# Block-sum DMAs of a hybrid decoder layer: half-size pieces at projection slots, copies on ScalarE's queue

## The chip, the cores and the metric

The kernel runs on one core of a Trainium2 chip. The metric is the device time of one execution in microseconds. The kernel before took 2511.54 us, the median of 2 runs (2511.51 to 2511.57).

The core has five engines that work side by side, each through its own instructions in order: TensorE (PE in the profile; PEld is its weight loads), VectorE (DVE), ScalarE (ACT), GpSimd (POOL) and SyncE (SP, which only issues DMAs here). DMAs are issued from the queue of an engine; the transfers themselves run on 16 DMA engines.

## The reference

One decoder layer over 2048 tokens of width 1024, with 16 learned meta tokens in front:

```python
u = _rmsnorm(h, norm_pre[layer])
proj = u @ w_in                      # split into 12 parts
att = _swa_sink_branch(a_q, a_k, a_v, attn_sinks)      # window 128, rotary, sinks
y_a = (att * silu(a_z)) @ w_attn_out
cell = _mlstm_cell(m_q, m_k, m_v, m_i, m_f)            # chunkwise recurrence
hm = _head_layernorm(sigmoid(m_o) * cell, head_norm)
y_m = (hm * silu(m_z)) @ w_mlstm_out
merged = sigmoid(g_a) * y_a + sigmoid(g_m) * y_m
h = h + _rmsnorm(merged @ w_out, norm_post[layer])
```

The code above is shortened; the projections are float32 and are computed to that accuracy from split operands (below).

## The kernel before

The kernel has two parts. The **projection part** takes the tokens in two halves of 1024 (`for c in range(NHALF)`, line 820). For each half it goes through 14 entries of `PLAN` (line 828): "A" entries project queries, keys and values of a group of heads for 8 blocks of 128 tokens, "F" entries project features (q and k of the mLSTM, or the gate `ga`), "M" entries project values and output gates of an mLSTM head. Every float32 operand is split into a high and a low part (`whi`, `wlo` for weights, `un` for tokens), and each product is three matmuls; `load_w` (line 217) loads the weights of an entry as `wraw` from SyncE's queue and splits them on ScalarE and VectorE (lines 229 to 235). A projection of one block is 24 matmuls. After every 6 of them, and at the end, it calls `slot()` (line 318), which counts a clock and lets waiting chains (attention blocks, mLSTM blocks, gates) put their next instructions in. When the queue of attention blocks is too long, `slot()` is also called without matmuls between. TensorE's order is the order of the code; the other engines' order is set by a scheduler that takes instructions by priority when it believes that their inputs are ready.

The **product part** (from line 966) computes six products of 2048x1024 by 1024x1024 (gates `az`, `mz`, `gm`, then `att`, `hm`, `out`), each by Winograd's form of Strassen's scheme: 7 products of half-size blocks instead of 8. That needs sums of weight blocks and of token blocks, the **block sums**. They are formed in DRAM during the projection part, by DMAs alone. `weight_sums()` (line 182) makes four blocks of 1 MB for each of the six matrices (`sw_d`): a copy `cp` from the weights `wq` or from another sum, then an accumulating DMA `add` onto it. `token_sums(c)` (line 165) does five accumulating DMAs on the token blocks `uo_d[c]`. The token blocks are written by `tokens()` (line 738): for each of 8 slices of tokens the scaled slice, and for some a negated copy made on ScalarE in a staging tile `xs` of four, is stored from SyncE's queue (lines 752 and 756).

Before, copies go through SyncE's queue and additions through POOL's. A copy is preceded by a transfer of one column of the newest weight tile `wlo` into its target (line 187), so that it can't be issued before that tile exists. One step of `weight_sums` (2 or 4 transfers of 1 MB) is put in at each entry of the plan (`next(sums, None)`), one of `token_sums` at entries 4, 6 and 8. Gate maxima of a half are stored to `mr_d` (line 395), and each mLSTM block loads its row of them, broadcast to all partitions, as `mrep` (line 608) from SyncE's queue.

Of the kernel before, what the change touches and what calls it, by code (L numbers as in the profile page):

```python
# [14 lines left out]
ALU = mybir.AluOpType  # L15
# [8 lines left out]
SB = 512  # L24
# [64 lines left out]
def hybrid_layer(ctx: ExitStack, tc: tile.TileContext, x, xT, mx, mxT, gpre, w_all, wq, negs, cw, cb,  # L89
                 gbias, hnorm, gpost, rope, ident, sel, bmask, out):  # L90
    nc = tc.nc
    V, S, G, T = nc.vector, nc.scalar, nc.gpsimd, nc.tensor
# [21 lines left out]
    def f(t):  # L114
        return t.bitcast(F32)
# [27 lines left out]
    def late_consts():  # L143
        for t, src in ((sink_t, negs.partition_broadcast(128)), (bm_t, bmask), (sel_t, sel),
# [16 lines left out]
    sw_d = [[dram.tile([128, 4 * SB], F32, name=f"sw{m}{i}_d") for i in range(4)] for m in range(len(MATS))]  # L161
    op_d = {(n, c): [dram.tile([128, 4, SB], F32, name=f"op_{n}{c}{i}_d") for i in range(7)]
            for n in ("att", "hm", "mg") for c in range(SEQ // (2 * SB))}

    def token_sums(c):
        b00, b10, t2, t1, t3, b11, t4, n01 = uo_d[c]

        def add(dst, src):
            G.dma_start(out=dst, in_=src, accum_op=ALU.add, max_dma_last_dim=4096)

        add(t1, n01)
        add(t3, n01)
        add(t2, b00)
        yield
        add(t2, n01)
        yield
        add(t4, t2)
        yield

    block_w = [None]  # L180

    def weight_sums():
        for a in range(0, len(MATS), 2):
            pair = (a, a + 1)

            def cp(dst, src):
                nc.sync.dma_start(out=dst[:, 0:1], in_=f(block_w[0])[:, 0:1])
                nc.sync.dma_start(out=dst, in_=src)

            def add(dst, src):  # L190
                G.dma_start(out=dst, in_=src, accum_op=ALU.add, max_dma_last_dim=4096)

            for m in pair:
                cp(sw_d[m][2], wq[m, 0, 0])
                cp(sw_d[m][0], wq[m, 1, 1])
            yield
            for m in pair:
                add(sw_d[m][2], wq[m, 0, 1])
                add(sw_d[m][0], wq[m, 0, 1])
            yield  # L200
            for m in pair:
                cp(sw_d[m][1], sw_d[m][2])
            yield
            for m in pair:
                add(sw_d[m][1], wq[m, 1, 1])
            yield
            for m in pair:
                cp(sw_d[m][3], sw_d[m][1])
            yield
            for m in pair:  # L210
                add(sw_d[m][3], wq[m, 1, 0])
            yield

    seq = [0]
    extra = [None]
# [42 lines left out]
    with es1:  # L258
# [54 lines left out]
        clock = [0, 0]  # L313

        def spawn(gen, delay=0):
            active.append([clock[0] + delay, gen])

        def slot():
            clock[0] += 1
            if queue and clock[0] >= clock[1] and clock[0] % SLOTS == CHAIN_PHASE:  # L320
                spawn(queue.pop(0))
                clock[1] = clock[0] + gap[0]
            for ch in list(active):
                if ch[0] <= clock[0]:
                    try:
                        ch[0] = clock[0] + next(ch[1])
                    except StopIteration:
                        active.remove(ch)

        def drain(all_=False):  # L330
            while queue or (all_ and active):
                slot()
# [432 lines left out]
        def token_proj(us, o, wh, wl, w, ps=None):  # L765
            if ps is None:
                ps = ps_p.tile([128, SB], F32, name="pj")
            n = 0
            for k in range(KT):
                for a, ww in ((0, wh), (0, wl), (1, wh)):  # L770
                    T.matmul(ps[:, :w], lhsT=us[k][:, a, o:o + 128], rhs=ww[k][:, :w],  # L771
                             start=(n == 0), stop=(n == 3 * KT - 1))
                    n += 1
                    if n % SLOT == 0 and n < 3 * KT:
                        slot()
            return ps
# [25 lines left out]
        rsn = [None] * SBH  # L802
        u = [None, None]
        late = None
        sums = weight_sums()

        def first_proj(us, wh, wl, w):
            banks = [ps_p.tile([128, SB], F32, name="pj") for _ in range(2)]
# [11 lines left out]
        for c in range(NHALF):  # L820
# [7 lines left out]
            for pi, (kind, arg, cols) in enumerate(PLAN):  # L828
                w = len(cols)
                if c == 0 and pi == 0:  # L830
# [13 lines left out]
                    wh, wl = load_w(w_all, off, w, each)  # L844
                else:
                    wh, wl = load_w(w_all, off, w, lead=100 if c == 0 and pi == 1 else SPLIT_LEAD)
                off += D * w
                block_w[0] = wl[0]
                if c or pi > 1:
                    next(sums, None)  # L850
                if pi in (4, 6, 8):
                    if pi == 4:
                        usums = token_sums(c)
                    next(usums)
                if c == 0 and pi == 0:
                    raw_x[1] = raw_tiles(SB, True)
                    early_consts()
# [283 lines left out]
    for n in range(N):  # L1141
        u, i = divmod(n, NP)
        nm, c, key = SETS[u]
# [95 lines left out]
```

## Time and profile before

| what | us |
|---|---|
| median of 2 runs | 2511.54 |
| the profiled execution | 2515.96 |
| its span, first to last instruction | 2514.2 |
| TensorE busy in the span | 2318.2 |
| ScalarE busy | 1110.6 |
| POOL busy | 573.9 |
| mean granted clock of TensorE | 0.957 of full speed |

The span is what the profile's other views divide up; 1.8 us of the profiled execution lie around it. A window of the profile gives for each engine the time in which it was busy, TensorE's mean granted clock, the mean busy share of the 16 DMA engines and the bytes that they moved. "Landing" is the time from a DMA's issue to the arrival of its data. The chain is followed back from the last instruction, at each step to what released it.

### The profile page before, as it was taken

To read this page: it belongs to the slowest core of one execution; us is meant where nothing else is said; L and a number is where in the kernel's file an instruction comes from. 1 tells how busy PE (TensorE), PEld (TensorE's weight loads), DVE (VectorE), ACT (ScalarE), POOL (GpSimd) and SP (SyncE) were. 2 spreads that over 40 slices of the span, in tenths; PEclk is the share of its full clock that TensorE was granted. 3 is DMA by queue.
4 is the path that set the end of the run, shared out by engine and by line. 5 is a ranking of instruction groups with operands and counts; after the bars stand their busy time and mean duration, and the time that the engine had idled before them with its cause. 6 is when DMAs were issued, how large, how long until landed. Compare 5 with 4: busy or idle time off the path is not lost.

```text
span 2514.2 us, 34052 instructions
## 1 busy us (share of the span) xinstructions
PE 2318.2 (92%) x11149; PEld 1956.4 (78%) x11149; DVE 1597.7 (64%) x3435; ACT 1110.6 (44%) x2721; POOL 573.9 (23%) x1185
## 2 busy tenths in 40 slices
PE   7688899998896899899998998999999999989897
PEld 7577788878785778788887787778878888877686
DVE  6655764575773586675575864765586454666775
ACT  6433543444452445454454553434544453333343
POOL 5234332343331434333434431000000000000010
PEclk8899999999997899899998999999999999999999
DMA  6943333741539754112111115877787677889974
GB/s 218 272 95 104 112 96 108 186 101 34 139 91 259 175 144 112 51 58 84 52 49 44 51 42 200 284 221 233 246 281 224 208 247 251 265 268 298 297 260 151
DMA packets 213683, 415.53 MB, mean 165 GB/s; under 512 B 25740, under 2 KB 83424, under 8 KB 213120
## 3 DMA queue, kind: packets, MB, share of 16 engines
q1 hardware_dynamic: 204256, 377.69, 46.3%
q0 software_dynamic: 9248, 35.65, 7.5%
q8 instruction: 88, 1.44, 0.2%
q14 instruction: 91, 0.75, 0.1%
HBM read 302.06 MB, written 172.01 MB: 189 GB/s over the span
## 4 chain that ended last, share of the span: by engine, by line
PE 55%; DVE 15%; DMA 14%; ACT 5%; POOL 5%; issue 5%; SPq 1%; ACTq 0%; DVEq 0%; POOLq 0%
PE x L1164 22%; PE pj L771 14%; PE pj L783 10%; PE acc L536 3%; DMA raw<-uo_d 3%; DVE wlo L235 2%; DMA mrep<-mr_d 2%; DMA wraw<-in_w_all 2%; PE s L484 2%; DVE xs L548 1%; DMA ld<-gm_d 1%; DVE st L986 1%; PE acc L604 1%; POOL pp L519 1%; POOL pc L522 1%
## 5 line engine op out<-in xcount | busy, mean ns | idle before, releaser
L1164 PE MATMUL x<-r,st 128*128 128x512 f32 x2688 | 622.8, 394 | 26.2 <-DVE ld L1130 9.3
L771 PE MATMUL pj<-whi,un 128*128 128x512 f32 (+2 forms) x1952 | 633.5, 382 | 0.0
L1164 PEld LDWEIGHTS x<-r,st 128*128 128x128 f32 x2688 | 511.9, 191 | 136.9 <-DVE st L986 9.6
L771 PEld LDWEIGHTS pj<-whi,un 128*128 128x128 f32 x1952 | 377.1, 195 | 40.7 <-issue 2.0
L771 PE MATMUL pj<-wlo,un 128*128 128x512 f32 (+2 forms) x976 | 367.7, 377 | 18.0 <-DVE wlo L235 18.0
L986 DVE TENSOR_TENSOR st<-raw,st 128x1024 fp32r<-128x1024 f32 x168 | 204.9, 1223 | 199.5 <-ACT st L985 197.9
L783 PE MATMUL pj<-un,whi 128*128 128x512 f32 x1024 | 328.5, 402 | 0.0
L1164 PE MATMUL x<-st,r 128*128 128x512 f32 x1344 | 309.0, 392 | 9.1 <-DVE st L986 5.3
L985 ACT CAST st<-raw 128x1024 fp32r<-128x1024 f32 x168 | 176.8, 1053 | 288.7 <-PE x L1164 151.5
L1164 PEld LDWEIGHTS x<-st,r 128*128 128x128 f32 x1344 | 253.6, 189 | 64.3 <-DVE st L986 6.0
L1072 POOL TENSOR_TENSOR yss<-yss,mhalf 128x1 f32<-128x1 f32 x16 | 12.6, 796 | 967.3 <-PE x L1164 889.5
L771 PEld LDWEIGHTS pj<-wlo,un 128*128 128x128 f32 x976 | 191.6, 196 | 39.2 <-DVE wlo L235 23.5
L783 PEld LDWEIGHTS pj<-un,whi 128*128 128x128 f32 x1024 | 188.6, 192 | 35.0
L493 ACT ACTIVATE P<-s,mn 128x144 f32<-128x144 f32 x256 | 95.3, 377 | 245.6 <-DVE mn L491 231.0
L783 PE MATMUL pj<-un,wlo 128*128 128x512 f32 x512 | 203.5, 397 | 0.0
L235 DVE TENSOR_TENSOR wlo<-wraw,whi 128x512 fp32r<-128x512 f32 (+3 forms) x224 | 140.8, 643 | 21.1 <-ACT whi L234 17.9
L986 DVE TENSOR_TENSOR r<-raw,r 128x1024 fp32r<-128x1024 f32 x66 | 80.6, 1223 | 94.3 <-ACT r L985 93.9
L234 ACT CAST whi<-wraw 128x512 fp32r<-128x512 f32 (+3 forms) x224 | 112.5, 531 | 34.1 <-DMA wraw<-in_w_all 18.9
L985 ACT CAST r<-raw 128x1024 fp32r<-128x1024 f32 x66 | 69.4, 1053 | 110.0 <-DMA raw<-sw_d 42.9
L484 PE MATMUL s<-ks,qs 128*128 128x272 f32 (+1 forms) x512 | 90.4, 298 | 28.7 <-ACT ks L465 25.9
L783 PEld LDWEIGHTS pj<-un,wlo 128*128 128x128 f32 x512 | 97.7, 191 | 22.0
L484 PEld LDWEIGHTS s<-ks,qs 128*128 128x128 f32 x512 | 81.2, 194 | 39.8 <-ACT ks L465 28.4
(363 smaller groups left out, 3527.6 us busy)
## 6 DMA issues: line engine op xcount, KB each, us to landing
raw<-sw_d SPq DMA_DIRECT2D x72, 512.0 KB, 5.6
raw<-in_wq SPq DMA_DIRECT2D x54, 512.0 KB, 4.7
wraw<-in_w_all SPq DMA_DIRECT2D x96, 256.0 KB, 3.2
sw_d<-in_wq POOLq DMA_DIRECT2D x24, 1024.0 KB, 13.3
raw<-uo_d SPq DMA_DIRECT2D x28, 512.0 KB, 5.1
raw<-op_att_d SPq DMA_DIRECT2D x28, 512.0 KB, 5.6
raw<-op_hm_d SPq DMA_DIRECT2D x28, 512.0 KB, 5.5
raw<-op_mg_d SPq DMA_DIRECT2D x28, 512.0 KB, 5.6
```

What stands on the lines that cost most here:

```text
L234: S.copy(hi[:, :w], raw[:, :w])
L235: tt(lo[:, :w], raw[:, :w], f(hi)[:, :w], ALU.subtract)
L484: T.matmul(sp[:, pa, c0:272], lhsT=qs[:, pr, pa, :], rhs=ks[:, i, c0:272], start=(i == 0), stop=(i == 1))
L493: S.activation(P[:, 2 * pa + pr], sp[:, pa, 128:272], AF.Exp, bias=mn[:, 2 * pr + pa:2 * pr + pa + 1], scale=-1.0, accum_out=mn[:, 4 + 2 * ...
L519: G.affine_select(pp[:, i], f(pc)[:, i], pattern=[[0, 4], [-1, 128]], compare_op=ALU.is_gt, fill=0.0, base=0, channel_multiplier=1)
L522: G.affine_select(pc[:, i], f(pc)[:, i], pattern=[[0, 4], [1, 128]], compare_op=ALU.is_ge, fill=0.0, base=0, channel_multiplier=-1)
L536: T.matmul(acc, lhsT=l, rhs=r.rearrange("p s q -> p (s q)"), start=(i == 0), stop=(i == len(ops) - 1))
L771: T.matmul(ps[:, :w], lhsT=us[k][:, a, o:o + 128], rhs=ww[k][:, :w], start=(n == 0), stop=(n == 3 * KT - 1))
L783: T.matmul(ps, lhsT=ww[k][:, 128 * i:128 * i + 128], rhs=us[k][:, a], start=(n == 0), stop=(n == 3 * KT - 1))
L985: S.copy(op[:, 0], raw)
L986: tt(op[:, 1], raw, f(op)[:, 0], ALU.subtract)
L1164: T.matmul(banks[bset][g], lhsT=l, rhs=r, start=(fresh and p == 0 and kk == 0 and m == 0), stop=(p == 1 and kk == 1 and m == 2), skip_grou ...
```

## The change

The block sums are cut in halves of 0.5 MB, `[128, 2 * SB]` of each block. Both generators yield after every piece, and `slot()` itself takes the next piece at every fifth call from the 80th on. The pieces of a half's token sums are put ahead of the rest when entry 4 of its plan begins. Copies are issued from ScalarE's queue (`S.dma_start`). Copies and additions are kept behind the instruction that was written before them on their engine (`tc.keep_in_program_order`). The transfer of one `wlo` column ahead of a copy is gone. Sums and their order of additions stay as they were: 24 copies, 24 additions of weights and 10 of tokens become 48, 48 and 20.

```diff
+    pin = tc.keep_in_program_order
+
+    def cp(dst, src):
+        pin(S.dma_start(out=dst, in_=src))
+
+    def add(dst, src):
+        pin(G.dma_start(out=dst, in_=src, accum_op=ALU.add, max_dma_last_dim=4096))
+
     def token_sums(c):
         b00, b10, t2, t1, t3, b11, t4, n01 = uo_d[c]
-        add(t1, n01)
-        add(t3, n01)
-        add(t2, b00)
-        yield
-        add(t2, n01)
-        yield
-        add(t4, t2)
-        yield
+        for dst, src in ((t1, n01), (t3, n01), (t2, b00), (t2, n01), (t4, t2)):
+            for j in range(2):
+                add(dst[:, 2 * j:2 * j + 2], src[:, 2 * j:2 * j + 2])
+                yield
...
-            def cp(dst, src):
-                nc.sync.dma_start(out=dst[:, 0:1], in_=f(block_w[0])[:, 0:1])
-                nc.sync.dma_start(out=dst, in_=src)
...
+            for op, i, src in ((cp, 2, (0, 0)), (cp, 0, (1, 1)), (add, 2, (0, 1)), (add, 0, (0, 1)),
+                               (cp, 1, 2), (add, 1, (1, 1)), (cp, 3, 1), (add, 3, (1, 0))):
+                for m in pair:
+                    for j in range(2):
+                        cs = slice(j * 2 * SB, (j + 1) * 2 * SB)
+                        v = sw_d[m][src] if isinstance(src, int) else wq[m, src[0], src[1]]
+                        op(sw_d[m][i][:, cs], v[:, cs])
+                        yield
...
         def slot():
             clock[0] += 1
+            if clock[0] >= 80 and clock[0] % 5 == 0 and sums:
+                if next(sums[0], 1) is not None:
+                    sums.pop(0)
...
-                block_w[0] = wl[0]
-                if c or pi > 1:
-                    next(sums, None)
-                if pi in (4, 6, 8):
-                    if pi == 4:
-                        usums = token_sums(c)
-                    next(usums)
+                if pi == 4:
+                    sums.insert(0, token_sums(c))
```

TensorE's order stays the same. What moves is shown at three places, before and then after; the same code has line numbers that are 22 lower after in `load_w` and 17 lower in the functions behind `slot()`. The first is SyncE's queue where the first mLSTM head's weights (`wraw`, 384 or 512 columns) and its gate maxima are loaded, in the first half. Before:

```order
L187 DMA sw_d<-wlo 128x1 x4
L229 DMA wraw<-in_w_all 128x384
L188 DMA sw_d<-in_wq 16x16384 x2
L229 DMA wraw_1299<-in_w_all 128x512
L188 DMA sw_d<-in_wq 16x16384
L395 DMA mr_d<-xs 36x128
L188 DMA sw_d<-in_wq 16x16384
L608 DMA mrep<-mr_d 128x128
L229 DMA wraw_2126<-in_w_all 128x384
L229 DMA wraw<-in_w_all 128x384 x3
L229 DMA wraw_2150<-in_w_all 128x384
L608 DMA mrep<-mr_d 128x128
```

The same place after:

```order
L207 DMA wraw<-in_w_all 128x512 x3
L207 DMA wraw<-in_w_all 128x384
L207 DMA wraw_1299<-in_w_all 128x512
L207 DMA wraw_2118<-in_w_all 128x384
L378 DMA mr_d<-xs 36x128
L207 DMA wraw<-in_w_all 128x384
L591 DMA mrep<-mr_d 128x128
L207 DMA wraw<-in_w_all 128x384 x2
L207 DMA wraw_2142<-in_w_all 128x384
L591 DMA mrep<-mr_d 128x128
L207 DMA wraw_2148<-in_w_all 128x384
L207 DMA wraw<-in_w_all 128x384
```

The four copies (`sw_d<-in_wq`) and their column transfers are gone from between the weight loads, the store `mr_d` and the loads `mrep`; everything else is in nearly the same order.

The second is SyncE's queue where the token blocks of the second half begin to be stored (`uo_d`), behind the last gate stores of the first half (`ga_d`). Before:

```order
L187 DMA sw_d<-wlo 128x1
L188 DMA sw_d<-in_wq 16x16384 x2
L797 DMA ga_d<-xs 128x512
L669 DMA hm_d<-tho 128x2x128
L187 DMA sw_d<-wlo 128x1 x2
L229 DMA wraw<-in_w_all 128x256
L188 DMA sw_d<-in_wq 16x16384
L797 DMA ga_d<-xs 128x512
L543 DMA att_d<-ao 128x2x128
L188 DMA sw_d<-in_wq 16x16384
L797 DMA ga_d<-xs 128x512
L752 DMA uo_d<-qT 128x512 x4
```

The same place after:

```order
L207 DMA wraw<-in_w_all 128x256
L780 DMA ga_d<-xs 128x512
L652 DMA hm_d<-tho 128x2x128
L780 DMA ga_d<-xs 128x512
L652 DMA hm_d<-tho 128x2x128
L780 DMA ga_d<-xs 128x512
L526 DMA att_d<-ao 128x2x128
L780 DMA ga_d<-xs 128x512
L735 DMA uo_d<-qT 128x512 x4
L735 DMA uo_d<-kT 128x512 x4
L735 DMA uo_d<-v_8325 128x512
L739 DMA uo_d<-xs 128x512
```

The four copies and their column transfers (three of which are in these rows) are gone from ahead of the stores `uo_d`, and the gate stores follow each other more closely.

The third is POOL's queue in the second half. Before, where three of that half's five token additions (`uo_d<-uo_d`) stand among the instructions of attention (`ropa`, `ropb`, `pp`, `pc`, `pmb`):

```order
L169 DMA uo_d<-uo_d 256x1024 x2
L502 TENSOR_TENSOR Pm<-P,mn 128x64
L303 TENSOR_TENSOR ropa<-qkv,rope 128x96
L304 TENSOR_TENSOR ropb<-qkv,rope 128x6x8
L305 TENSOR_TENSOR ropb<-qkv,rope 128x6x8
L306 TENSOR_TENSOR qkv<-ropa,ropb 128x6x16
L169 DMA uo_d<-uo_d 256x1024
L519 AFFINE_SELECT pp<-pc 128x512 x2
L522 AFFINE_SELECT pc<-pc 128x512 x2
L528 TENSOR_TENSOR pmb<-pm,bm 128x512
L303 TENSOR_TENSOR ropa<-qkv,rope 128x96
L304 TENSOR_TENSOR ropb<-qkv,rope 128x6x8
```

After, where the two halves of one of these additions stand, some way later in the program, among attention and mLSTM instructions:

```order
L450 CAST ks<-km_194 128x2x16
L502 AFFINE_SELECT pp<-pc 128x512
L596 MEMSET v_12018 128x2x2
L597 MEMSET v_12018 128x1
L502 AFFINE_SELECT pp<-pc 128x512
L505 AFFINE_SELECT pc<-pc 128x512 x2
L511 TENSOR_TENSOR pmb<-pm,bm 128x512
L583 TENSOR_TENSOR cs<-cst_202,cs 128x257
L171 DMA uo_d<-uo_d 128x1024
L645 TENSOR_TENSOR msm<-msm,mhalf 128x1
L619 AFFINE_SELECT dw<-dw 128x128
L171 DMA uo_d<-uo_d 128x1024
```

An addition moves half the rows, the additions stand further apart, and they have moved from the attention blocks of one entry to those of later entries.

## Rows read from the trace of the kernel before

**Rows 1.** The page: span, engines, chain by engine, one group (busy, mean ns)

```profile
span 2514.2 us, 34052 instructions
...
PE 2318.2 (92%) x11149; PEld 1956.4 (78%) x11149; DVE 1597.7 (64%) x3435; ACT 1110.6 (44%) x2721; POOL 573.9 (23%) x1185
...
PE 55%; DVE 15%; DMA 14%; ACT 5%; POOL 5%; issue 5%; SPq 1%; ACTq 0%; DVEq 0%; POOLq 0%
...
L771 PE MATMUL pj<-whi,un 128*128 128x512 f32 (+2 forms) x1952 | 633.5, 382 | 0.0
```

**Rows 2.** Windows: length, busy PE, PEld, DVE, ACT, POOL; clock, DMA share, GB/s

```profile
90.00:160.00 70.00, 46.92 (x211) 36.27 (x209) 36.56 (x108) 24.27 (x73) 14.98 (x33) 0.83 0.86 207
210.00:230.00 20.00, 15.48 (x92) 14.65 (x91) 11.04 (x26) 6.64 (x28) 12.22 (x28) 1.00 0.61 119
500.00:540.00 40.00, 34.20 (x178) 27.93 (x177) 28.89 (x80) 20.04 (x63) 17.09 (x34) 0.96 0.61 156
600.00:640.00 40.00, 29.78 (x142) 26.23 (x141) 20.96 (x54) 14.31 (x53) 16.73 (x35) 0.79 0.04 11
670.00:690.00 20.00, 16.17 (x90) 13.14 (x89) 17.63 (x41) 10.44 (x30) 5.88 (x13) 1.00 0.34 104
770.00:810.00 40.00, 16.94 (x60) 13.33 (x59) 12.59 (x24) 9.83 (x23) 5.77 (x9) 0.66 1.04 301
860.00:880.00 20.00, 10.99 (x45) 10.09 (x44) 3.73 (x10) 4.12 (x13) 7.94 (x15) 0.74 0.78 146
880.00:920.00 40.00, 35.79 (x162) 27.60 (x162) 32.40 (x85) 18.96 (x49) 11.81 (x23) 0.96 0.76 204
920.00:1000.00 80.00, 79.62 (x451) 70.65 (x450) 58.57 (x187) 42.63 (x143) 34.63 (x80) 1.00 0.32 88
0.00:1540.00 1540.00, 1386.81 (x7117) 1190.88 (x7117) 985.53 (x2639) 715.81 (x2180) 561.36 (x1169) 0.94 0.40 111
```

**Rows 3.** Timeline of SyncE, 100 to 110 us: start, length, line, transfer

```profile
100.06 0.37 SPq L395 DMA_DIRECT2D mr_d<-xs  x1
...
108.88 0.36 SPq L608 DMA_DIRECT2D mrep<-mr_d  x1
109.33 6.67 SPq L229 DMA_DIRECT2D wraw<-in_w_all  x5
```

**Rows 4.** Chain in order of time, 70 to 1000 us: start, length, what

```profile
89.88 17.31 issue
...
770.85 20.59 DMA uo_d<-qT
```

**Rows 5.** Timeline of ScalarE near 217 and 790 us; bracketed: idle before, releaser

```profile
217.73 0.59 ACT L538 COPY xs<-acc 64x512 f32<-64x512 f32 x1 [0.35 <-PE acc L536]
...
780.09 0.63 ACT L755 ACTIVATE xs<-v 128x512 f32<-128x512 f32 x1 [3.49 <-DMA ga_d<-xs]
...
789.97 0.63 ACT L755 ACTIVATE xs<-dws 128x512 f32<-128x512 f32 x1 [8.59 <-DMA ga_d<-xs]
...
801.87 0.60 ACT L796 ACTIVATE xs<-pj 128x512 f32<-128x512 f32 x1 [10.76 <-DMA uo_d<-xs]
```

**Rows 6.** Timeline of POOL near 867 us

```profile
866.82 0.90 POOL L169 DMA_DIRECT2D uo_d<-uo_d  x1 [9.41 <-DMA uo_d<-uo_d]
```

**Rows 7.** Tile sw_d: issues, duration ns min/median/max, first and last start

```profile
L1012 SPq DMA_DIRECT2D raw<-sw_d x72: 319/320/731, 1545.1 to 2386.0; - x72
...
L191 POOL DMA_DIRECT2D sw_d<-in_wq x24: 877/951/1552, 107.9 to 993.2; - x24
```

**Rows 8.** DMA issues: transfer, count, KB each, median us to landing

```profile
raw<-sw_d SPq DMA_DIRECT2D x72, 512.0 KB, 5.6
...
sw_d<-in_wq POOLq DMA_DIRECT2D x24, 1024.0 KB, 13.3
...
wraw<-in_w_all SPq DMA_DIRECT2D x64, 128.0 KB, 2.1
...
uo_d<-qT SPq DMA_DIRECT2D x4, 256.0 KB, 20.3
```

More of the change, by code (lines that the diff above doesn't have):

```diff
@@ L163, in hybrid_layer @@
             for n in ("att", "hm", "mg") for c in range(SEQ // (2 * SB))}
+    pin = tc.keep_in_program_order
[3 more added lines that the diff above has]
+        pin(G.dma_start(out=dst, in_=src, accum_op=ALU.add, max_dma_last_dim=4096))
     def token_sums(c):
         b00, b10, t2, t1, t3, b11, t4, n01 = uo_d[c]
-        def add(dst, src):
-            G.dma_start(out=dst, in_=src, accum_op=ALU.add, max_dma_last_dim=4096)
-        add(t1, n01)
-        add(t3, n01)
-        add(t2, b00)
-        yield
-        add(t2, n01)
-        yield
-        add(t4, t2)
-        yield
-    block_w = [None]
+        for dst, src in ((t1, n01), (t3, n01), (t2, b00), (t2, n01), (t4, t2)):
+            for j in range(2):
+                add(dst[:, 2 * j:2 * j + 2], src[:, 2 * j:2 * j + 2])
+                yield
     def weight_sums():
@@ L184, in weight_sums @@
             pair = (a, a + 1)
-            def cp(dst, src):
-                nc.sync.dma_start(out=dst[:, 0:1], in_=f(block_w[0])[:, 0:1])
-                nc.sync.dma_start(out=dst, in_=src)
[L190 to L212, printed above, removed]
+            for op, i, src in ((cp, 2, (0, 0)), (cp, 0, (1, 1)), (add, 2, (0, 1)), (add, 0, (0, 1)),
[6 more added lines that the diff above has]
+                        yield
     seq = [0]
@@ L316, in spawn @@
             active.append([clock[0] + delay, gen])
+        sums = []
         def slot():
             clock[0] += 1
+            if clock[0] >= 80 and clock[0] % 5 == 0 and sums:
+                if next(sums[0], 1) is not None:
+                    sums.pop(0)
             if queue and clock[0] >= clock[1] and clock[0] % SLOTS == CHAIN_PHASE:
@@ L804, in hybrid_layer @@
         late = None
-        sums = weight_sums()
+        sums.append(weight_sums())
         def first_proj(us, wh, wl, w):
```

## The prediction

> **What bounds the kernel now.** I read the page first: TensorE is busy 92% of the span and holds 55% of the chain that ended last, DMA 14% [rows 1]. So a gain must be idle time of TensorE, or time at its lower clock. The table by windows comes second, because the change touches only the projection part. That part runs to about 1540 us, and TensorE is busy for 1386.81 of them [rows 2]: some 153 us are idle. Where the DMA share is moderate TensorE hardly waits: from 920 to 1000 us it is busy for 79.62 of 80 us at a share of 0.32. Where the share is near 1 it waits: 46.92 of 70 us from 90 to 160, 16.94 of 40 us from 770 to 810. Not all idle time goes with DMA: from 600 to 640 us it is idle for 10.2 us at a share of 0.04, where attention blocks are run out between two projections.
>
> The chain in order of time comes third; it names what was late. Among its longest pieces between 70 and 1000 us are 17.31 us of issue, which end where SyncE at last gets to the loads that stand behind the copies, and a store of 20.59 us [rows 4]. What is in the way there are the block sums: copies and accumulating DMAs of 1 MB, issued several at a time.
>
> **What each burst costs.** Idle time plus clock loss, from rows 2. An engine busy for b us at a mean granted clock g has lost (1-g)·b against full speed; the two levels are 1.2 and 2.4 GHz, and the lower one is seen after TensorE has idled.
> - A, 90 to 160: 23.1 idle, 0.17·46.92 = 8.0; 31.1.
> - F, 770 to 810: 23.1 idle, 0.34·16.94 = 5.8; 28.9.
> - G, 860 to 920: 9.0 + 4.2 idle, 2.9 + 1.4; 17.5.
> - The small ones, 210 to 230, 500 to 540, 670 to 690: 4.5 + 5.8 + 3.8 idle, 1.4 clock; 15.5.
> The sum is 93.0 us.
>
> **The change part by part.** *A goes almost whole.* There SyncE issues four 1 MB copies, each held until its small guard transfer has landed, and POOL issues its additions beside them. The store of the gate maxima goes out at 100.06 between two copies; the first load that reads it can be issued only at 108.88, and five loads of the next weights stand behind that one in SyncE's queue, from 109.33 [rows 3]. In the new order no copy stands there, and the first copy is on ScalarE near the place that ran at 217.7 us before [rows 5]. What remains is the store, the load that reads it and the last weights behind that load, 3·2.1 us by the smallest load row [rows 8], say 7 us, and 2 of clock. Back: 22 us.
>
> *F goes in part.* ScalarE waits 3.49, 8.59 and 10.76 us for its own staging tiles to be stored [rows 5], behind token stores that land in 20.3 us (median of four) [rows 8]; attention on TensorE waits for ScalarE. In the new order two half copies and two half additions stand just ahead, and no copy in SyncE's queue. But 16 stores of 256 KB still leave at once, and the first staging tile's is about the ninth: 9·0.262 MB at the 301 GB/s that this window moved is 7.8 us. So 8 us idle and 2 of clock stay; 19 come back.
>
> *G.* POOL sat 9.41 us before one addition that had to wait for an earlier one to land [rows 6], and the masks that attention needs stood behind it in POOL's queue. In the new order these additions come 100 to 260 us later and are spread out. 13 of 17.5 come back; the rest is the first maxima load of the second half. Of the small ones I take 10 of 15.5, as attention is run out around 210 us anyway, as it is from 600 to 640.
>
> Together 22 + 19 + 13 + 10 = 64 us.
>
> *What is added.* 24 copies become 48, on ScalarE's queue. One issue of the same shape took 320 ns, 731 at most [rows 7]: 15 to 35 us of ScalarE. Its share of the chain is 5% of 2514, 126 us of 1110.6 busy [rows 1], so about 11% of its time decides: 2 us; all of it exposed would be 35, none 0. 34 additions become 68. POOL spent 951 ns on one of 1 MB [rows 7]; half the size costs between half of that and all of it, so POOL gets 1 to 33 us more. Its share is 126 of 573.9 busy, 22%; of the middle, 17 us, 4 decide. Exposed whole it is 33, and 0 if all falls in POOL's idle time. 24 copies also wait on ScalarE for an addition to land. By the plan at least four pieces, 20 slots, lie between; a slot in a projection is six products of 382 ns [rows 1], so 46 us against 13.3 us for an addition of twice the size [rows 8]. I take 0; it cannot gain, and the upper end is 24·6.7 = 160 us, each held for half of 13.3. The DMAs of SyncE and ScalarE share eight completion semaphores in turn, so a load on SyncE can wait for a copy that ScalarE has not issued. I take 3 us; 0 if the copy is always early; at six places the two stand within 5 us of each other, by the trace's times of their neighbours, and a half-size transfer lands in 5.6 us [rows 8], so up to 34. SyncE loses 24 copies and 24 guards, which is counted in A and F.
>
> More, smaller transfers: loads of 128 and 512 KB landed in 2.1 and 5.6 us [rows 8], so about 0.9 us of each doesn't depend on size. 58 pieces more are 54 us of latency over 1000 us, and nobody waits for a piece within 46 us: 0, and 54 at most.
>
> Net 64 - 2 - 4 - 3 = 55. Against the profiled execution's 2515.96 us (span 2514.2 and 1.8 around it) that is 2461; the median of the runs shown is 4.4 us lower, so I say 2457 us, 2.2% faster.
>
> **Rivals.** *Give-back.* The same bytes cross the same 16 engines, so a stall only moves: the token stores and gate loads at A and F are late even alone, and pieces now meet loads that were undisturbed. For it: F's window holds 301 GB/s, much of it token stores. Against it: at a share of 0.32 nothing waits [rows 2]. Then only G's POOL wait and half of A return, 13 + 15 us, and the time is 2511.5 - 28 = 2484. The Trainium skill, "DMA: Bandwidth & Descriptors", Issuing engines are not separate DMA queues, says that a second issuing queue saves only issue time; this agrees with what I take for the move to ScalarE, which is nothing by itself.
>
> *Each piece pays its fixed time.* If the sums were a chain that something waits for, the 54 us of fixed latency would be added: 2457 + 54 = 2511, no change. Against it: the last sums are issued near 1250 us by the new order, and the part that reads them begins at 1540. The Trainium skill, "DMA: Bandwidth & Descriptors", Rules for kernel authors, speaks for it: it wants 1 MiB or more per DMA, and its Anatomy of one DMA puts some 2 us of fixed cost on each, 116 us for 58 pieces (an estimate from that page). The loads show half of that; no row shows it for an addition.
>
> *Pieces run clean.* All 93 come back, less 6 for the issues: 2425.
>
> *ScalarE is held.* ScalarE executes in order. If POOL is behind by more than the 46 us that the plan gives, each of the 24 dependent copies holds ScalarE for a landing of 6.7 us, and exponentials and splits stand behind it: 160 us, of which about half is covered, since ScalarE is busy 715.81 of 1540 us [rows 2]. 2511.5 - 55 + 80 = 2537, slower; it decides from 55/24 = 2.3 us per copy that nothing covers. For it: POOL is on attention's chain. Against it: the order puts 20 to 40 slots between, and POOL's own waits shrink.
>
> *It doesn't do what it says.* The scheduler may issue pieces early and together. In the new order they are spread but not even: two stand three instructions apart on POOL. If they clump, the give-back time holds.
>
> **How the numbers follow.** Forecast (2438 to 2478) 0.56, clean 0.09, give-back and clumping 0.24, fixed time 0.03, held 0.08. Faster by over 2% means under 2461.3 us; 2% is about what a measurement of this kernel tells from no change. The forecast gives 0.41 to faster and 0.15 to same, clean 0.09 to faster, give-back 0.03 and 0.21, fixed time 0.03 to same, held 0.02 to same and 0.06 to slower: 0.53, 0.41, 0.06. The range from 2425 to 2500 leaves out most of the held case, and the edges of the others.
>
> **What would show it.** Right: from 90 to 160 us TensorE is busy for over 60 us; the wait of ScalarE for its staging tiles near 770 us is under 10 us in all; no wait of POOL for its own DMA over 3 us; the clock is 1.0 there; the DMA share never stays near 1 outside the token stores; the part after the projections is the same length. Wrong: copies on ScalarE with idle time ahead, released by an addition; TensorE waiting for ScalarE or for POOL's masks near 220, 600 and 1010 us more than before; weight loads on SyncE released by a copy.

## The result, and the profile after

The changed kernel took 2478.4 us (median of two runs, 2478.31 to 2478.5) against 2511.54 before: a ratio of 0.9868, 95% interval 0.9826 to 0.991. That is 33 us or 1.3% faster, inside the range of 2425 to 2500 us and 21 us above the predicted 2457. By the bound of 2% it counts as no change, the second likeliest of the three. The two profiled executions differ a little more, by the spans 2514.2 - 2476.8 = 37.4 us, and the accounts below go by them.

From the page of the changed kernel (beside [rows 1]):

```profile
span 2476.8 us, 34095 instructions
...
PE 2309.2 (93%) x11149; PEld 1946.3 (79%) x11149; DVE 1591.3 (64%) x3435; ACT 1109.9 (45%) x2721; POOL 595.0 (24%) x1219
...
q1 hardware_dynamic: 200032, 352.51, 43.8%
q0 software_dynamic: 9792, 35.66, 9.9%
q10 hardware_dynamic: 6912, 25.17, 3.4%
...
PE 38%; DVE 12%; DMA 10%; ACT 4%; issue 3%; POOL 2%; SPq 0%; ACTq 0%; DVEq 0%; POOLq 0%
```

TensorE does the same 11149 products. New is q10, ScalarE's queue with the copies. q0 is POOL's queue with the additions: it moves what it moved before, but the DMA engines now spend 9.9% of the span on it, where the page of the kernel before has 7.5%:

```profile
q0 software_dynamic: 9248, 35.65, 7.5%
```

The shares of the chain sum to only 69%, so I don't compare them.

Windows of the changed kernel, columns as in [rows 2]. Everything comes some 20 to 50 us earlier now, so the windows from 770 us on hold other work than in [rows 2]:

```profile
90.00:160.00 70.00, 64.52 (x341) 52.60 (x340) 53.35 (x160) 32.85 (x105) 22.61 (x52) 0.98 0.15 44
250.00:300.00 50.00, 41.55 (x183) 33.15 (x182) 34.42 (x77) 25.98 (x69) 14.72 (x31) 0.90 0.50 120
450.00:500.00 50.00, 42.34 (x191) 33.35 (x191) 31.11 (x73) 26.20 (x71) 10.78 (x25) 0.90 0.52 134
770.00:810.00 40.00, 32.96 (x172) 29.19 (x170) 28.25 (x65) 20.70 (x60) 13.79 (x28) 0.96 0.74 215
0.00:1540.00 1540.00, 1418.78 (x7285) 1213.99 (x7286) 1007.66 (x2668) 739.36 (x2209) 582.36 (x1203) 0.96 0.47 119
```

In the first stage TensorE is busy for 64.52 of 70 us at clock 0.98, against 46.92 at 0.83. But there are two windows, at 250 and 450 us, in which it idles 8.5 and 7.7 us and the mean granted clock is 0.90. Before, at about the same place in the program, it was busy for 46.66 and 47.51 of 50 us, at nearly the same mean share of the DMA engines:

```profile
270.00:320.00 50.00, 46.66 (x220) 37.75 (x218) 36.63 (x81) 28.26 (x76) 15.07 (x33) 0.93 0.47 151
470.00:520.00 50.00, 47.51 (x241) 38.83 (x241) 35.71 (x86) 29.74 (x82) 12.21 (x30) 1.00 0.49 161
```

To compare by place and not by time, I matched every TensorE instruction of one trace with the same one of the other; its order is the same in both. The difference of their starts is the lead of the changed kernel, and where the lead grows or shrinks, time was won or lost:

```
program place, by the times before     lead at its ends    won (+) or lost (-)
   0 to 80                              0.0  ->  3.6         + 3.6
  80 to 160   (A)                       3.6  -> 29.4         +25.8
 160 to 260                            29.4  -> 30.5         + 1.1
 260 to 460                            30.5  -> 28.7         - 1.8  (at 280 to 300: -9.7)
 460 to 540                            28.7  -> 24.6         - 4.1  (at 480 to 520: -9.5)
 540 to 760                            24.6  -> 18.6         - 6.0
 760 to 860  (F)                       18.6  -> 36.5         +17.9
 860 to 960  (G)                       36.5  -> 47.8         +11.3
 960 to 1140                           47.8  -> 42.0         - 5.8
1140 to last product                   42.0  -> 40.1         - 1.9
```

The last 2.7 us of the lead go behind the last product. The three places where the change was to help gave 55.0 us. But 17.7 us were lost between and behind them (1.8, 4.1, 6.0 and 5.8), over stretches in which pieces now lie that were not there before.

What happened at one of these places, 250 to 275 us: ScalarE in the changed kernel, its bracket the idle time before and what ended it.

```profile
261.66 0.63 ACT L665 ACTIVATE xs<-xs 128x512 f32<-128x512 f32 x1 [2.35 <-DMA xs<-in_x]
...
268.42 0.63 ACT L665 ACTIVATE xs<-xs 128x512 f32<-128x512 f32 x1 [4.90 <-DMA xs<-in_x]
...
269.15 0.38 ACT L476 ACTIVATE P<-s,mn 128x144 f32<-128x144 f32 x1
```

TensorE at the same time:

```profile
263.98 0.39 PE L766 MATMUL pj<-un,wlo 128*128 128x512 f32 x1
270.04 1.13 PE L467 MATMUL s<-ks,qs 128*128 128x144 f32 x4 [5.67 <-ACT P L476]
```

And POOL's additions just ahead:

```profile
257.09 0.82 POOL L171 DMA_DIRECT2D uo_d<-uo_d  x1
...
258.49 0.81 POOL L171 DMA_DIRECT2D uo_d<-uo_d  x1 [0.22 <-issue]
```

ScalarE squares the second half's token rows as they are loaded (L665). Its program order puts the exponentials of attention (L476) behind these squares. A row that lands late, beside two additions, holds ScalarE for 4.90 us, the exponentials come late, and TensorE idles 5.67 us for them. The DMA issues of 240 to 275 us (KB each, median us to landing) in the changed kernel, then of 270 to 300 us in the kernel before:

```profile
xs<-in_x SPq DMA_DIRECT2D x8, 256.0 KB, 5.7
uo_d<-uo_d POOLq DMA_DIRECT2D x4, 512.0 KB, 7.9
wraw<-in_w_all SPq DMA_DIRECT2D x4, 256.0 KB, 5.1
```

```profile
xs<-in_x SPq DMA_DIRECT2D x8, 256.0 KB, 3.0
wraw<-in_w_all SPq DMA_DIRECT2D x5, 256.0 KB, 3.4
```

The loads are the same; beside additions they take 5.7 us in place of 3.0. That gave the theory of the experiments. **Theory 1:** a piece costs where it meets a load that an engine waits for in order; the additions are the ones that do it. **Theory 2:** ScalarE pays, for issuing the copies and for their waits. **Theory 3:** it is the size of the pieces.

### The profile page after: what moved, and what is told of

Read it like the earlier page. It is cut to its first block, busy times and chain, and to the rows that moved or that the text cites. A ratio compares the mean times of both kernels' runs of the same rounds, so it can differ in the third digit from the quotient of the medians.

```text
span 2476.8 us, 34095 instructions
## 1 busy us (share of the span) xinstructions
PE 2309.2 (93%) x11149; PEld 1946.3 (79%) x11149; DVE 1591.3 (64%) x3435; ACT 1109.9 (45%) x2721; POOL 595.0 (24%) x1219
## 3 DMA queue, kind: packets, MB, share of 16 engines
q0 software_dynamic: 9792, 35.66, 9.9%
## 4 chain that ended last, share of the span: by engine, by line
PE 38%; DVE 12%; DMA 10%; ACT 4%; issue 3%; POOL 2%; SPq 0%; ACTq 0%; DVEq 0%; POOLq 0%
PE x L1142 21%; PE pj L754 8%; PE pj L766 4%; DMA raw<-uo_d 3%; PE acc L519 2%; DVE xs L531 1%; DMA ld<-gm_d 1%; DVE st L964 1%; DMA wraw<-in_w_all 1%; DMA raw<-sw_d 1%; DVE r L964 1%; DVE wlo L213 1%; DVE e L1083 1%; PE s L467 1%; ACT r L963 1%
## 5 line engine op out<-in xcount | busy, mean ns | idle before, releaser
L476 ACT ACTIVATE P<-s,mn 128x144 f32<-128x144 f32 x256 | 95.3, 377 | 233.2 <-DVE mn L474 200.8
L502 POOL TENSOR_SCALAR_AFFINE_SELECT pp<-pc 128x512 fp32r<-128x512 f32 x120 | 78.7, 659 | 118.7 <-ACT pc L497 107.7
```

Source lines behind the costliest of these rows:

```text
L476: S.activation(P[:, 2 * pa + pr], sp[:, pa, 128:272], AF.Exp, bias=mn[:, 2 * pr + pa:2 * pr + pa + 1], scale=-1.0, accum_out=mn[:, 4 + 2 * ...
L502: G.affine_select(pp[:, i], f(pc)[:, i], pattern=[[0, 4], [-1, 128]], compare_op=ALU.is_gt, fill=0.0, base=0, channel_multiplier=1)
```

## The experiments

All ratios are to the kernel before, timed beside each run on the same chip.

**How much do the sums cost, and which half of them?** Two edits of the changed kernel (the second is the `add` line alone):

```diff
 def cp(dst, src):
-    pin(S.dma_start(out=dst, in_=src))
+    pass
 def add(dst, src):
-    pin(G.dma_start(out=dst, in_=src, accum_op=ALU.add, max_dma_last_dim=4096))
+    pass
...
-        v = sw_d[m][int(name[1]) - 1] if name[0] == "s" else wq[m, int(name[1]), int(name[2])]
+        v = wq[m, 0, 0] if name[0] == "s" else wq[m, int(name[1]), int(name[2])]
```

> Leaves out every copy and every addition of the block sums in the projection part; the products load an untouched block of the same size instead of a sum, so the loads of the product part stay. It shows what the sums cost the changed kernel in all. Theory 1 (pieces take the DMA engines from SyncE's loads, above all those of the second half's token rows, and ScalarE waits for them in order): the places that lost 38 us in sum after about 230 us give most of it back, 2440 us, 2430 to 2455. Rival (the sums are hidden by now, and what stays idle is the run-out of attention): within 8 us of the changed kernel, 2470 to 2480.

> Leaves out the 68 additions alone; the 48 copies stay on ScalarE's queue in their slots. Theory 1 (the accumulating pieces fill the DMA engines for 3.6 us each and loads behind them land late): most of what all sums cost comes back, the time is within 8 us of the kernel without any sums, about 2445 us. Theory 2 (ScalarE is held by issuing 48 copies at 0.49 us each and by their waits): most of the cost stays, 2470 to 2480 us.

Without sums: 2435.4 us, ratio 0.9675 (0.9653 to 0.9698). Without additions: 2441.7 us, 0.9704 (0.9689 to 0.9719). So the sums still cost the changed kernel 0.9868 - 0.9675, about 48 us, and 41 of these are the additions; the 48 copies on ScalarE, alone, cost 7. (The interval of the changed kernel's own ratio makes the first two uncertain by 10 us; the 7 are the difference of two ratios whose intervals overlap, so they may be anything from nothing to 14.) That the additions are the ones that cost holds; theory 2 falls as the main cause. By places, in the times of the run without sums, the changed kernel loses to it at 260 to 270 us (8.1), 440 to 470 (10.7), 750 to 780 (8.2), and small pieces elsewhere. The same account puts the kernel before 88 us above the one without sums (80 by the medians, as the profiled execution without sums was the fastest of its four), where the prediction had counted 93 us of idle time and clock loss.

**Is it the meeting with the loads?** Pieces pause while the second half's token rows are squared:

```diff
-            if clock[0] >= 80 and clock[0] % 5 == 0 and sums:
+            if clock[0] >= 80 and clock[0] % 5 == 0 and sums and \
+                    not (120 <= clock[0] < 142 or 232 <= clock[0] < 254):
```

> No piece is issued in slots 120 to 141 and 232 to 253, where ScalarE squares the second half's token rows as they are loaded; these pieces follow later. Theory 1: ScalarE's waits for these loads (24.1 us in five) go to under 8 us, as before the change, the two places that lost 9.7 and 9.5 us (at 250 to 280 and 455 to 505 us) lose under 3 each, and the time is 2463 us, 2457 to 2470. Theory 2 (issue and waits of copies on ScalarE): as many copies as ever, 2474 to 2482 us.

2463.2 us, ratio 0.9788 (0.9771 to 0.9804), 20 us less than the changed kernel by the ratios (and 19.3 by the spans, 2476.8 against 2457.5), for keeping pieces out of 44 slots. The waits of ScalarE from 60 to 1500 us (total, times, longest), in the changed kernel:

```profile
ACT whi L212 <- DMA wraw<-in_w_all: 26.0, 15, 6.0
ACT xs L665 <- DMA xs<-in_x: 24.1, 5, 8.8
...
ACT P L476 <- DMA sw_d<-sw_d: 7.1, 2, 3.8
```

with the pause:

```profile
ACT whi L212 <- DMA wraw<-in_w_all: 25.8, 18, 5.6
ACT xs L666 <- DMA xs<-in_x: 7.5, 2, 4.1
```

and without sums:

```profile
ACT whi L212 <- DMA wraw<-in_w_all: 12.0, 14, 2.0
...
ACT xs L665 <- DMA xs<-in_x: 8.5, 3, 4.7
```

The wait for token rows goes from 24.1 to 7.5 us, to what is there without any sum; the wait for weights, which the pause was not made for, stays (26.0, then 25.8), and is 12.0 without sums. (The third row of the changed kernel, a wait for one of the sums' own transfers, is misleading; the part "A version for time" below shows why.) The rows of tokens land in 2.8 us again, from 240 to 275 us:

```profile
xs<-in_x SPq DMA_DIRECT2D x8, 256.0 KB, 2.8
```

In the same two windows as above the clock is at 1.00 with the pause, and over the projections the DMA engines' mean share is what it was (0.48 against 0.47):

```profile
250.00:300.00 50.00, 46.59 (x238) 38.24 (x237) 40.61 (x98) 30.22 (x83) 14.65 (x34) 1.00 0.35 91
450.00:500.00 50.00, 47.40 (x247) 39.18 (x246) 40.07 (x98) 30.21 (x86) 13.38 (x31) 1.00 0.36 92
0.00:1540.00 1540.00, 1423.24 (x7345) 1220.70 (x7346) 1015.27 (x2673) 747.63 (x2218) 581.88 (x1203) 0.96 0.48 122
```

The first place now loses 0.7 us against before, the second still 4.8 us, which is more than the 3 expected. The pieces and their bytes are the same as in the changed kernel; none lies in these 44 slots, and those behind come later. By the account by place, 9.5 and 4.7 us of the 19.3 were won at the two places themselves, the rest elsewhere. So for these places theory 1 is shown: some 14 us of the 48 are the meeting with the loads of token rows.

**Is it the accumulation, or POOL's issuing?** POOL's pieces as plain copies:

```diff
-        pin(G.dma_start(out=dst, in_=src, accum_op=ALU.add, max_dma_last_dim=4096))
+        pin(G.dma_start(out=dst, in_=src, max_dma_last_dim=4096))
```

> POOL's 68 pieces are plain copies and accumulate nothing: as many issues on POOL in the same slots, the same bytes written, nothing read back at the destination. Theory 1 with the accumulation as the price (3.6 us of the 16 engines per piece against 1.75 for a copy of its size): the queue's share falls from 9.9 to about 5 per cent and at least half of the 37 us that the additions cost comes back, 2460 us or less, ratio 0.979 or less. Rival (POOL's 0.84 us for each issue, with attention's masks behind it, is the price): ratio stays at 0.985 to 0.989.

2458.3 us, ratio 0.9773 (0.9735 to 0.9811). The queue row of that run's page:

```profile
q0 software_dynamic: 9792, 35.66, 5.2%
```

As many packets, the same bytes, half the share: 5.2% of 2451.9 us over 68 pieces is 1.9 us of all 16 engines for a plain piece, against 9.9% of 2476.8 over 68, 3.6 us, for an accumulating one. Of the additions' 0.0164 this gives back 0.0095, a good half, some 24 us with an uncertainty of 14. The accumulation itself is thus a large part of the price, but two things fell with it: the time for which a piece takes the DMA engines, and POOL's issue, which took 579 ns per plain piece of the weight sums in place of 845 (POOL's busy time 576.7 us in place of 595.0). The rival, POOL's issue, is therefore not excluded by this run. What a plain piece still costs, 0.0069 or 17 us, is issue on POOL and the plain copy's own traffic; these two were not parted either.

**Queue and size, one at a time and together.** The first edit sends copies out on SyncE's queue again; the second makes pieces of 1 MB, one per ten slots; the third is both, which leaves of the change the placement alone:

```diff
-    pin(S.dma_start(out=dst, in_=src))
+    pin(nc.sync.dma_start(out=dst, in_=src))
```

```diff
-            for j in range(2):
-                add(dst[:, 2 * j:2 * j + 2], src[:, 2 * j:2 * j + 2])
-                yield
+            add(dst, src)
+            yield
...
-                    for j in range(2):
-                        cs = slice(j * 2 * SB, (j + 1) * 2 * SB)
...
-                        op(sw_d[m][i][:, cs], v[:, cs])
-                        yield
+                    op(sw_d[m][i], sw_d[m][src] if isinstance(src, int) else wq[m, src[0], src[1]])
+                    yield
...
-            if clock[0] >= 80 and clock[0] % 5 == 0 and sums:
+            if clock[0] >= 80 and clock[0] % 10 == 0 and sums:
```

> The changed kernel with its 48 copies issued from SyncE's queue in the same slots (the move to ScalarE undone). Theory 1 (what costs is where the accumulating pieces land): the queue matters little, ratio to before within 0.004 of the changed kernel's 0.987, some 2474 to 2488 us. Rival (ScalarE pays for issues and waits of the copies): ScalarE's issue goes and the time falls by 5 to 15 us, ratio 0.981 to 0.985. Second rival (SyncE is what must stay free): loads stand behind copies again and the time rises by 10 us or more, ratio 0.991 or above.

> Pieces of 1 MB, one per ten slots, in place of half of it per five; queue, start and order of the sums as in the changed kernel. Theory 1: the same bytes meet the same loads, fewer times and longer, and POOL and the DMA engines are spared the second half's fixed share (queue share back from 9.9 to near 7.5 per cent): 2478 us, within 6. Theory 3 (the piece's size is what makes the difference, small ones let loads through): 2490 to 2505 us.

> Of the change only the placement: pieces of 1 MB, one per ten slots in program order, copies on SyncE's queue, no guards. Neither the halves nor ScalarE's queue alone moved the time by more than 0.4 per cent; if they don't matter together either, the ratio to before is 0.983 to 0.991, some 2480 us. If one of the two is needed (SyncE's loads stand behind 24 copies of 1 MB), 0.995 or above.

Queue undone: 2473.8 us, 0.9834 (0.9801 to 0.9867). Size undone: 2483.7 us, 0.9869 (0.985 to 0.9887). Both undone: 2463.0 us, 0.9789 (0.9761 to 0.9818). The first two are within what theory 1 expected; but 0.9834 lies as well in the range of the rival, that ScalarE pays for its copies, so the first does not tell them apart. The third is a miss: better than either bound, and 20 us better than the whole change by the ratios. Theory 3 in the form "small pieces let loads through" falls: 1 MB pieces are no slower on ScalarE's queue and seem faster on SyncE's (0.9789 against 0.9834, intervals that just overlap). Of the change, then, the placement wins some 53 us, and the halves and the move to ScalarE together give 20 back. The second run also says that the DMA engines' time is not the whole price: with 1 MB pieces POOL's queue took 7.9% of the span in place of 9.9% and POOL was busy for 573.9 us in place of 595.0, and the time stayed (0.9869 against 0.9868). A longer piece may then cost more where it meets a load; no run shows it by itself.

Why ScalarE's queue is worse for 1 MB pieces (0.9869 against 0.9789) is not settled. Of the 27 us by which the two traces part, 6.0 lie at one place, 450 to 460 us, where SyncE with the copies on ScalarE's queue waits for an earlier weight load to land before it issues the next ones:

```profile
SPq L203 <- DMA wraw<-in_w_all: 6.6, 1, 6.6
```

The Trainium skill, "DMA: Bandwidth & Descriptors", Queues, rings and completion order, says that each DMA engine takes turns between the queues that have work; a copy on a third queue would then take turns with the loads, where on SyncE's queue it stands in line ahead of or behind them. No run here isolates that, and the landings at this place don't bear it out: from 440 to 460 us the seven weight loads of 256 KB landed in 6.9 us (median) with the copies on ScalarE's queue and in 9.7 with them on SyncE's.

**The move of the copies without the placement.** In the kernel before:

```diff
 def cp(dst, src):
-    nc.sync.dma_start(out=dst[:, 0:1], in_=f(block_w[0])[:, 0:1])
-    nc.sync.dma_start(out=dst, in_=src)
+    S.dma_start(out=dst, in_=src)
```

> The kernel before with one part of the change alone: its 24 copies of 1 MB go out from ScalarE's queue without the small guard transfers; additions, sizes and places stay. If SyncE's queue behind copies and guards was what cost 31 us from 90 to 160 us, most of that comes back and little else, 2490 us, ratio 0.988 to 0.995. If the bytes cost it there, whichever queue issues them: within 6 us of before, ratio 0.997 to 1.003.

2599.1 us, ratio 1.0335 (1.0295 to 1.0376): 3.4% slower, and both expectations missed. The guards had been what kept the copies in their place. Without them the scheduler sends the first one out at the very start, and ScalarE is held by copies that wait for additions. The tile of the weight sums and the waits of ScalarE up to 320 us in that run:

```profile
L190 POOL DMA_DIRECT2D sw_d<-in_wq x24: 869/917/1578, 12.7 to 298.2; - x24
L187 ACTq DMA_DIRECT2D sw_d<-in_wq x12: 496/501/606, 0.8 to 239.8; - x12
```

```profile
ACT whi L233 <- DMA wraw<-in_w_all: 70.8, 16, 16.6
ACT tho L617 <- DMA sw_d<-in_wq: 31.5, 3, 19.0
ACT P L492 <- DMA sw_d<-in_wq: 25.4, 2, 13.2
```

All additions of weights go out by 298 us instead of 993 [rows 7]. ScalarE stands 56.9 us before copies that wait, and 70.8 us for weights. So the rival "ScalarE is held" does occur, in a kernel that doesn't keep the pieces in their slots; how much of the 86 us is this and how much the late weights was not parted. Because the edit moved the copies as well, this run says nothing on how A's 25.8 us divide between queue and bytes.

**A version for time.** Pieces stay away from the weight loads at both sides of each projection's start (the list `starts` of their slots, not shown here, as is the counter `last`), from the token rows, and from the token stores of the second half:

```diff
-            if clock[0] >= 80 and clock[0] % 5 == 0 and sums:
+            if 80 <= clock[0] and clock[0] >= last[0] + 3 and sums and not (
+                    any(-8 <= clock[0] - s_ <= 6 for s_ in starts) or 120 <= clock[0] < 142 or
+                    232 <= clock[0] < 254 or 404 <= clock[0] < 425):
+                last[0] = clock[0]
```

> A version for time: pieces as in the changed kernel, at least three slots apart, and none from eight slots before the start of a projection to six behind it (where its weights are loaded), none while the second half's token rows are squared (as in the run with the pause), and none while its tokens are split and stored (slots 404 to 424). Theory 1: what the pause left, about 30 us above the kernel without sums, shrinks to 15; ratio 0.970 to 0.976, some 2445 us. If a load that is not of the weights or tokens is what remains (gate maxima, staging), the pieces only move into it: ratio 0.977 to 0.982.

2451.7 us, ratio 0.9746 (0.9713 to 0.978), as expected. ScalarE's wait for weights fell to 17.9 us. The next experiments rest on the second of these rows, which I read as three waits for an addition:

```profile
ACT whi L212 <- DMA wraw<-in_w_all: 17.9, 15, 5.4
ACT P L482 <- DMA sw_d<-in_wq: 12.2, 3, 4.7
```

That reading is wrong. The first of the three, ScalarE and then VectorE:

```profile
205.73 0.50 ACTq L168 DMA_DIRECT2D sw_d<-in_wq  x1
210.59 0.38 ACT L482 ACTIVATE P<-s,mn 128x144 f32<-128x144 f32 x1 [4.28 <-DMA sw_d<-in_wq]
...
210.34 0.16 DVE L480 TENSOR_TENSOR mn<-mn,negs 128x2 f32<-128x2 f32 x1
```

ScalarE issued its copy without a wait, and the first addition of weights was issued only at 217.7 us. What the exponential waited for is `mn` of VectorE, done at 210.50; the copy merely landed at about that time, and the profile puts the wait down to it. The same exponential waits as long in the kernel without any sums:

```profile
207.66 0.38 ACT L476 ACTIVATE P<-s,mn 128x144 f32<-128x144 f32 x1 [4.19 <-DVE mn L474]
```

The other two are alike (3.22 and 4.68 us, 3.22 and 3.87 without sums), and so are the waits of this kind in the changed kernel (4.13, 3.84 and 3.22 us; 4.19, 3.84 and 3.22 without sums). In this run no copy had ScalarE idle ahead of it; in the changed kernel one had, for 1.4 us.

On the wrong reading, each step was then done for all six matrices before the next (`for a in range(0, len(MATS), 6)`, `pair = tuple(range(a, a + 6))`), with three forms of the pieces: halves on ScalarE's queue, halves on SyncE's, and 1 MB at least six slots apart on ScalarE's.

> As the run with the shielded loads, and each step is done for all six matrices before the next one, so that between an addition and the copy that reads it stand twelve pieces or more in place of four. ScalarE's three waits there for an addition to land (12.2 us) go to zero. If they are exposed, the ratio falls from 0.975 to 0.969 to 0.973, some 2440 us; if attention run-out hides them, it stays within 0.002 of 0.975.

> The same with copies on SyncE's queue: within 0.004 of the run beside it with copies on ScalarE, whichever sign. If ScalarE's 48 issues of about 0.49 us matter, 5 us or more faster.

> The same on ScalarE's queue with pieces of 1 MB, at least six slots apart. POOL's queue share falls from 10.0 to about 7.9 per cent, as it did with 1 MB per ten slots. Theory 1 with occupancy as the price: the DMA engines are taken for less in all, 0 to 6 us faster than in halves. If a load that meets a longer piece loses more, 4 us or more slower.

Halves: 2448.3 us, 0.9729 (0.9707 to 0.9752), and on SyncE's queue 2446.1 us, 0.9724 (0.9697 to 0.975): the row of waits shows 3.8 us in one where it showed 12.2 in three, but none of it was a wait for an addition, and 0.9729 against 0.9746 is within the intervals, so the order of the steps is not shown to matter. With the loads shielded the queue makes no difference. With 1 MB: 2434.9 us, 0.9675 (0.9649 to 0.9701), 13 us better than halves and more than the 6 expected. That is the ratio of the kernel that leaves the sums out: they cost nothing that could be told from zero any more, to within some 6 us. Larger pieces also halve the issues on POOL and ScalarE (POOL was busy for 577.9 us against 601.3 with halves), so how much of the 13 us is the DMA engines' time is open. Queue and wait rows of that run:

```profile
q0 software_dynamic: 9248, 35.65, 8.0%
```

```profile
ACT whi L208 <- DMA wraw<-in_w_all: 15.9, 18, 2.2
...
ACT xs L667 <- DMA xs<-in_x: 6.4, 3, 3.5
```

No wait for weights is over 2.2 us, as without sums (2.0). Here the trace agrees with the Trainium skill, "DMA: Bandwidth & Descriptors", Rules for kernel authors, which wants 1 MiB or more per DMA for the most bandwidth: 0.9675 against 0.9729. The changed kernel's own slots show no such gain on ScalarE's queue (0.9869 against 0.9868).

## Why the prediction was right and where it was wrong

**The stages that the change was made for: right.** The prediction took 22, 19 and 13 us for A, F and G, 54 in all; the places gave 25.8, 17.9 and 11.3, 55.0. The signs it named came too: over 60 us busy from 90 to 160 (64.52), and no wait of ScalarE for staging tiles near 770 [rows 5] is left among its waits from 740 to 860 us. The clock came near its sign (0.98 from 90 to 160 us, 0.96 from 770 to 810, where it said 1.0). POOL waited once for 4.1 us with an addition, at 1165 us, but not for a transfer of its own: it waited for a copy from ScalarE's queue to land (`sw_d<-sw_d`), a wait that the prediction did not count.

**The small places and the added costs: wrong, and that is the whole miss.** The prediction took 10 us back at the small places, 2 + 4 + 3 us for the additions of work, a net gain of 1. Outside A, F and G the projections won 3.6 and 1.1 us and lost 17.7: a net loss of 13.0. With 1.9 us lost from there to the last product and 2.7 behind it, 17.6 are lost where 1 was to be won; less the 1 us that A, F and G gave beyond their 54, that is the whole distance from the predicted 55 to the 37.4 of the spans.

**The step that failed** is the argument against the give-back, that at a DMA share of 0.32 nothing waits [rows 2]. A mean over 80 us was taken for what a single load meets. The runs show that what counts is whether a piece stands beside a load that an engine waits for in order: pieces kept away from two such places for 44 slots are worth 14 us there, and 20 in all, at nearly the same mean share. The give-back time of 2484 us was nearer to the result than the forecast, though not by its own account, which let A and F give back their gain; they kept it, and others paid.

**The prices of single pieces.** The copies on ScalarE were taken at 320 to 731 ns each; they took 498 (from the inputs) and 477 ns (between sums), and all 48 cost 7 us in sum with their traffic, where 2 were taken for issue and 3 for shared semaphores. The price of a copy's issue was to be had from the kernel before, in the view of [rows 7], in place of the loads' 320 ns:

```profile
L188 SPq DMA_DIRECT2D sw_d<-in_wq x12: 488/500/602, 90.3 to 769.2; - x12
L188 SPq DMA_DIRECT2D sw_d<-sw_d x12: 467/474/530, 200.7 to 985.6; - x12
```

That the move to ScalarE's queue is nothing by itself did not hold for pieces of 1 MB in the changed kernel's slots (20 us between the queues); for halves the difference is within the intervals. The additions on POOL were to cost between half and all of 951 ns: they took 845 ns in the median, so half the size saves POOL little, and its busy time rose by 595.0 - 573.9 = 21.1 us (17 were taken; the bounds of this term were written as 1 to 33 us, but 68 issues at half of 951 ns are no more than 34 at 951, so they are 0 to 32). But the price of the halves that the prediction did not have at all is on the DMA engines: 9.9% of the span against 7.5%, 245 us against 189, for the same bytes. A landing that nobody waits for was costed at nothing; the engines' time that it takes from others was left out. How much of the 48 us goes to this and how much to POOL's issues stays open, as said above.

**The rivals.** *ScalarE is held*: it was not. Of the 48 copies one had ScalarE idle ahead of it for over half a microsecond, 1.4 us at 731.6 us, so the nothing that was taken for copies that wait for additions was right. *Fixed time per piece*: the last addition was issued at 1202.9 us and the part that reads the sums began at some 1500, so nobody waited for the sums at their end. The Trainium skill, "DMA: Bandwidth & Descriptors", Anatomy of one DMA, states its 2 us for DMAs issued from GpSimd, which only 34 of the 58 pieces are. *Pieces run clean*: the changed kernel did not come near 2425; the placement away from the loads in 1 MB pieces did, with 2434.9. *It doesn't do what it says*: it does; the pieces are spread out, from 164.2 to 1202.9 us.

## What to carry to other kernels

Work in the background that nobody waits for is still paid by whatever shares its resource; look in the trace for the loads that an in-order engine waits for, and place the transfers between them rather than evenly. An average share of the DMA engines says nothing on that. Don't cut accumulating transfers smaller to be gentle: here the halves took the engines longer, and 1 MB pieces, kept away from the loads, cost nothing that could be measured. And before a wait is believed that the profile puts down to a transfer, look for the same instruction in a run without that transfer: three waits here were there without it too.

## What was not expected of the hardware

An accumulating transfer between two places in DRAM takes the DMA engines about twice as long as a plain one: 3.6 us of all 16 engines for 512 KB against 1.9 us for a plain copy from the same queue (9.9% and 5.2% in the rows above). In halves, the same bytes took 9.9% instead of 7.5%. The number of packets does not explain it: of the 9792 and 9248 packets 8704 are of 4096 bytes in both traces, and the rest have 4 bytes. It is these 8704 that took longer, 447 ns each on average in place of 345; in the runs with 1 MB pieces in slots it was 361 (one per ten) and 358 ns (shielded), so it goes with the halves and not with the slots. Why is open: a half here is a cut of columns, 4096 of each row's 8192 bytes, and halves cut by rows were not tried. And POOL needs nearly as long to issue half a megabyte (845 ns) as a whole one (951 ns [rows 7]; 917 ns in the run with the copies moved alone).
